# Reading the moving tile and writing the PSUM bank from the last column to the first, in the weight matmuls of a hybrid decoder layer

## The chip, the core and the metric

The kernel runs on one core of one Trainium2 chip. The metric is the device time of one execution in microseconds (us). The kernel before takes 705.18 us, the median of three runs (705.11 to 707.22 us).

## What is computed

One decoder layer over 512 tokens of width 1024, float32 in and out. Cut to what matters here:

```python
h = rms_norm(x, mix_norm_g)
proj = h @ w_in                      # 1024 x 3864
u, q, kv, nsa_g, merge_g = split(proj)
y_pool = pooling_mixer(u, pool_w, pool_scale) @ w_pool_out
y_nsa = nsa_mixer(q, kv, ...) @ w_nsa_out
x = x + (gate_pool * y_pool + gate_nsa * y_nsa) @ w_out
h = rms_norm(x, ffn_norm_g)
gate_pre, val = split(h @ w_up)      # 1024 x 5632
gate_c = causal_dwconv(gate_pre, conv_w, conv_b)
x = x + (silu(gate_c) * val) @ w_down   # 2816 x 1024
```

The products with `w_in`, `w_pool_out`, `w_nsa_out`, `w_out`, `w_up` and `w_down` are dense and take most of the arithmetic. The sparse attention inside `nsa_mixer` is computed as dense causal attention with masks, beside a compressed branch.

## The kernel before, in words

**Layout.** Activations lie transposed: 128 features on the partitions, 512 tokens along the free dimension. A dense product takes a 128x128 block of weights as the stationary operand and a 128x512 tile of activations as the moving operand, and adds up over the blocks of the contraction in one PSUM bank of 512 float32 columns.

**Three products for one.** Each float32 operand is split into a rounded part (names ending in `h` or `hi`) and the rest (`l`, `lo`), both of type fp32r. One block of the contraction is three matmuls: high weights by high activations, high by low, low by high. `mm3` (lines 439 to 446) issues these three for each block `k` into one bank `pt`. `weights` (lines 424 to 434) brings the weights from DRAM through the ring `wraw` and splits them into the rings `whi` and `wlo`, either with ScalarE (ACT) and VectorE (DVE), or with ACT and a DMA that adds on GpSimd's queue (POOL).

**Who calls `mm3`.** `feature` (22 outputs of `w_in`, 8 blocks each), `pool_out` (8 outputs, 4 blocks), the product with `w_nsa_out` (8 outputs, 4 blocks), the product with `w_out` (8 outputs, 8 blocks), `up_plain` (the first 4 of the 22 blocks of the feed-forward width, 2 outputs of 8 blocks each), `dn_group` (4 groups of 8 outputs, 4 blocks each) and the last product (8 outputs, 6 blocks). Each of these matmuls is 512 columns wide.

**Who calls `product`.** For the other 18 blocks of the feed-forward width, `up_fast` (from line 1178) computes the two outputs by a scheme that needs seven products of half width in the place of eight. `product` (lines 1133 to 1141) issues one of them: 4 blocks, three matmuls each, 256 columns wide, into the first 256 columns of a bank. Sums of weights are made on DVE beforehand; the moving tiles `nh`, `nl`, `th`, `tl` are sums and differences of the normalised activations, made once by `halves`.

**What else PE does.** TensorE (PE) also runs ten warm-up matmuls on a tile of ones, the projections `round_a` and the value projection (weights as the moving operand), the four matmul triples of `mix`, the compression matmuls (moving tile `kcb`, read with a step of 8 elements, 62 columns), attention scores, transposes and the products with the values (`av`). None of these is touched.

**What sets the order.** All instructions are first noted in a plan (`Plan.note`), then put in an order per engine by a small simulation (`Plan.run`) with a price for each instruction (`Plan.price`: for PE it is worked out from the number of columns of the moving operand alone) and with the dependences that `_span` finds from the footprint of every access pattern. `_span` takes steps below zero into account. `emit` then issues the instructions, all from line 382, so that every row of the profile reads L382 and groups are told apart by the names of their tiles: `mm<-xh,whi` writes a bank with the tag `mm` from the moving tile `xh` and the weights `whi`. The feed-forward weights come on SyncE's DMA queue (SP).

Of the kernel before, what the change touches and what calls it, by code (L numbers as in the profile page):

```python
# [385 lines left out]
def hybrid_layer(ctx: ExitStack, tc: tile.TileContext, xT, pos, par, cst, poolw, w1, wa, wb, wf,  # L386
# [3 lines left out]
    PE, ACT, DVE, POOL, SP = pl.engines  # L390
# [16 lines left out]
    def keep(name, shape, dt=F32, bufs=1):  # L407
        return pl.tile(sb, shape, dt, name, "t_" + name, bufs)

    def bank(tag, shape=(P, T)):  # L410
        return pl.tile(ps, shape, F32, tag, tag, {"mm": 2, "tr": 3, "av": 1, "sc": 1}[tag], psum=True)
# [12 lines left out]
    def weights(ap, width, lo="d"):  # L424
        raw, hi, low = ring("wraw"), ring("whi", F32R), ring("wlo", F32R)
        SP.dma_start(raw[:, :width], ap)
        if lo == "d":
            ACT.activation(low[:, :width], raw[:, :width], AF.Copy, scale=-1.0)
            POOL.dma_start(low[:, :width], raw[:, :width], accum_op=ALU.add)
            ACT.activation(hi[:, :width], raw[:, :width], AF.Copy)  # L430
        else:
            ACT.activation(hi[:, :width], raw[:, :width], AF.Copy)
            DVE.tensor_sub(low[:, :width], raw[:, :width], f32(hi[:, :width]))
        return hi, low

    def flat(ap):
        return ap.rearrange("p k n -> p (k n)")

    def mm3(pt, wh, wl, xh, xl, k0, k1, koff=0, nk=None, first=0):
        nk = k1 if nk is None else nk  # L440
        for k in range(k0, k1):
            c = slice((k - koff) * P, (k - koff + 1) * P)
            with pl.unit():
                PE.matmul(pt, wh[:, c], xh[k], start=(k == first), stop=False)
                PE.matmul(pt, wh[:, c], xl[k], start=False, stop=False)
                PE.matmul(pt, wl[:, c], xh[k], start=False, stop=(k == nk - 1))

    def rsqrt(dst, v, tmp):
        y, a = dst, tmp
# [32 lines left out]
    pt = bank("mm")  # L482
# [3 lines left out]
    xr, xh, xl = [None] * KD, [None] * KD, [None] * KD  # L486
# [113 lines left out]
    for c, (k0, k1) in enumerate(((0, 3), (3, 6), (6, 8))):  # L600
        raw = ring("wraw")
        SP.dma_start(raw[:, :(k1 - k0) * 280], flat(wb[:, k0:k1]))
        for j in range(k1 - k0):
            home = ("pp", 10) if len(bw) < 5 else ("pt", 6)
            hi, lo = (pl.tile(sb, (P, 280), F32R, n, home[0], home[1]) for n in ("bh", "bl"))
            split(hi, lo, raw[:, j * 280:(j + 1) * 280])
            bw.append((hi, lo))
    for t in range(NT):
        pt = bank("mm")
        tk = slice(t * P, (t + 1) * P)  # L610
        for k in range(KD):
            wh, wl = bw[k]
# [46 lines left out]
    for t in range(NT):  # L659
        x, y = qp[t], kp[t]  # L660
# [33 lines left out]
    def feature(i, hi, lo):  # L694
        wh, wl = weights(flat(wf[i]), 1024)
        pt = bank("mm")
        mm3(pt, wh, wl, hi, lo, 0, KD)
        return pt
# [8 lines left out]
    with pl.on("f"):  # L707
        for i in range(2):
            pt = feature(i, xh, xl)
# [48 lines left out]
        def pool_out(c):  # L758
            wh, wl = weights(wpo[c].rearrange("p a k n -> p (a k n)"), 1024)
            for f in (2 * c, 2 * c + 1):  # L760
                o = (f % 2) * 512
                pt = bank("mm")
                mm3(pt, wh[:, o:o + 512], wl[:, o:o + 512], yph, ypl, 0, 4)
                DVE.scalar_tensor_tensor(gpy[f], gpy[f], 1.0, pt, op0=ALU.add, op1=ALU.mult)
                SP.dma_start(gdr[f], gpy[f])
# [25 lines left out]
    for i in range(2):  # L791
# [4 lines left out]
        pt = bank("tr")  # L796
# [20 lines left out]
    x = keep("kcx", (64, 1, DH))  # L817
# [195 lines left out]
    def any_bank():  # L1013
        turn[0] += 1
        return bank(("mm", "tr", "tr", "mm", "tr", "av")[turn[0] % 6])

    mh, ml, nots = [], [], []
    for c in range(4):
        wh, wl = weights(wno[c].rearrange("p a k n -> p (a k n)"), 1024, "v")
        for f in (2 * c, 2 * c + 1):  # L1020
            o = (f % 2) * 512
            pt = any_bank()
            mm3(pt, wh[:, o:o + 512], wl[:, o:o + 512], Oh, Ol, 0, 4)
            nots.append(pl.last())
            m = page("tn")
            with pl.behind(tail):
                SP.dma_start(m, tdr[f])
            DVE.scalar_tensor_tensor(m, m, 1.0, pt, op0=ALU.add, op1=ALU.mult)
            gp = page("gp")
            with pl.behind(tail):  # L1030
                SP.dma_start(gp, gdr[f])
            DVE.tensor_add(m, m, gp)
            hi, lo = page("mh", dt=F32R), page("ml", dt=F32R)
            ACT.activation(hi, m, AF.Copy, scale=0.5)
            DVE.scalar_tensor_tensor(lo, m, 0.5, f32(hi), op0=ALU.mult, op1=ALU.subtract)
            mh.append(hi)
            ml.append(lo)
            if f > 1:
                tail = nots[f - 2]
# [4 lines left out]
    for f in (0, 4, 1, 5, 2, 6, 3, 7):  # L1044
        xres = page("xres")
        with pl.behind(tail):
            SP.dma_start(xres, xT[f])
        wh, wl = weights(flat(wout[f]), 1024, "v")
        pt = any_bank()
        mm3(pt, wh, wl, mh, ml, 0, KD)  # L1050
        tail = pl.last()
        x2[f] = pl.tile(sb, (P, T), F32, "x2", "pp", 10)
        DVE.tensor_add(x2[f], pt, xres)
        gh[f], gl[f] = page("gh", dt=F32R), page("gl", dt=F32R)
        split(gh[f], gl[f], x2[f], ffng[:, f:f + 1])
        if f:
            sq = page("sq")
            ACT.activation(sq, x2[f], AF.Square)
            DVE.tensor_add(acc, acc, sq)
        else:  # L1060
            ACT.activation(acc, x2[f], AF.Square)
# [3 lines left out]
    H2 = T // 2  # L1065
# [67 lines left out]
    def product(bank_, a, b, k0):  # L1133
        ah, al = a
        bh, bl = b
        for k in range(4):
            c = slice(k * P, (k + 1) * P)
            with pl.unit():
                for j, (w, x) in enumerate(((ah, bh), (ah, bl), (al, bh))):
                    PE.matmul(bank_[:, :H2], w[:, c], x(k), start=k0 and k == 0 and j == 0,  # L1140
                              stop=k == 3 and j == 2, skip_group_check=True)

    def mov(i, half):
# [34 lines left out]
    def up_fast(f, n1, n2, n3):  # L1178
# [30 lines left out]
        p1, u2, u3 = half[0][:, :H2], half[0][:, H2:], half[1][:, :H2]  # L1209
        g, y = page("fg"), page("y")  # L1210
        product(bx, halves_(a1, 0), mov(0, 0), True)
        begun.append(pl.last())
        ACT.activation(p1, bx[:, :H2], AF.Copy)
        more = list(held)
        del held[:]
        if more:
            more[0]()
        fill(n1, f == PLAIN)
        product(by, h2, mov(2, 1), True)
        DVE.tensor_add(u2, by[:, :H2], p1)  # L1220
        if more:
            more[1]()
        fill(n3)
        product(bq, h1, mov(2, 0), True)
        product(bx, halves_(a1, 1), mov(1, 0), False)
        ACT.activation(g[:, :H2], bx[:, :H2], AF.Copy)
# [31 lines left out]
    for f in range(8):  # L1258
        wh, wl = weights(flat(wdz[f]), 768, "v")
        pt = any_bank()  # L1260
# [99 lines left out]
```

## Time and profile before

| | us |
|---|---|
| Median of three runs | 705.18 |
| The profiled execution | 706.15 |
| Its span, from the first to the last instruction | 704.4 |
| PE busy in it | 697.2 |
| LDWEIGHTS (PEld) busy, beside PE | 615.6 |
| DVE busy | 492.7 |
| ACT busy | 422.3 |
| POOL busy | 103.7 |

The profiled execution is 0.97 us above the median of the runs, and 1.75 us of it lie outside the span. A busy share says how much of the span an engine had an instruction in flight. [...] What a matmul costs in a dense row is the distance from its start to the next start. This is called its pace below.

### The profile page before, as it was taken

The page shows a single profiled execution, that of the slowest core. Times are in us where ns is not written, and L with a number is a line of the kernel's source. Part 1 is how long each engine was busy: PE and PEld are TensorE (multiplying, and loading weights), DVE is VectorE, ACT ScalarE, POOL GpSimd, SP SyncE. Part 2 cuts the span into 40 slices and gives each one's busy share as a digit, 9 for nine tenths or more (in the row PEclk, how much of TensorE's full clock was granted, in tenths as well). Part 3 has the DMA queues.
Part 4 walks back from the last instruction along what each step waited for, and adds up shares of the span by engine and source line. Part 5 has one row for each costly group of instructions (what it writes and reads, how often), then busy time and mean ns, then how long its engine had stood idle before and what let it go on. Part 6 is the DMA issues. An engine that isn't in the chain of part 4 may idle for free.

```text
span 704.4 us, 11308 instructions
## 1 busy us (share of the span) xinstructions
PE 697.2 (99%) x4142; PEld 615.6 (87%) x4142; DVE 492.7 (70%) x1060; ACT 422.3 (60%) x756; POOL 103.7 (15%) x127
## 2 busy tenths in 40 slices
PE   9999999999999999999999999999999999999997
PEld 8898888888888888888888899999989999999886
DVE  6768488887866653675569967886778777776632
ACT  8557367677776664333467857685757566673310
POOL 0001301010110000000021323231312112220000
PEclk9999999999999999999999999999999999999999
DMA  8477255454565567844369698989868666774131
GB/s 297 167 180 224 61 120 135 105 132 109 150 153 143 146 139 229 280 158 156 122 150 235 151 211 170 219 185 222 186 173 205 157 162 166 170 161 112 45 127 60
DMA packets 45272, 113.99 MB, mean 162 GB/s; under 512 B 5281, under 2 KB 5409, under 8 KB 45217
## 3 DMA queue, kind: packets, MB, share of 16 engines
q1 hardware_dynamic: 29232, 76.57, 33.6%
q0 software_dynamic: 15840, 36.71, 29.1%
q8 instruction: 32, 0.52, 0.3%
q14 instruction: 24, 0.19, 0.1%
q10 hardware_dynamic: 144, 0.01, 0.0%
HBM read 70.27 MB, written 6.29 MB: 109 GB/s over the span
## 4 chain that ended last, share of the span: by engine, by line
PE 88%; DMA 3%; issue 3%; DVE 3%; ACT 1%; POOL 1%; POOLq 0%; ACTq 0%; DVEq 0%
PE mm L382 39%; PE tr L382 28%; PE sc L382 12%; PE av L382 10%; DMA sl<-r 2%; DMA r<-wup 1%; DVE wlo L382 1%; DMA sl<-wraw 0%; ACT whi L382 0%; DVE y L382 0%; POOL tl L382 0%; POOL sl L382 0%; ACT ft L382 0%; ACT sh L382 0%; DVE kc L382 0%
## 5 line engine op out<-in xcount | busy, mean ns | idle before, releaser
L382 ACT ACTIVATE whi<-wraw 128x1024 fp32r<-128x1024 f32 (+1 forms) x96 | 97.9, 1019 | 74.4 <-issue 29.0
L382 DVE TENSOR_TENSOR wlo<-wraw,whi 128x1024 fp32r<-128x1024 f32 (+1 forms) x66 | 76.4, 1157 | 16.6 <-ACT whi L382 14.3
L382 POOL DMA_DIRECT2D wlo<-wraw x30 | 26.3, 875 | 332.0 <-ACT wlo L382 278.7
L382 PE MATMUL mm<-xh,whi 128*128 128x512 f32 x176 | 73.0, 415 | 0.3
L382 PE MATMUL mm<-xh,wlo 128*128 128x512 f32 x176 | 69.0, 392 | 0.0
L382 PE MATMUL mm<-xl,whi 128*128 128x512 f32 x176 | 69.0, 392 | 0.0
L382 PE MATMUL mm<-tl,sh 128*128 128x256 f32 x190 | 53.8, 283 | 0.0
L382 PE MATMUL mm<-th,sh 128*128 128x256 f32 x174 | 49.5, 285 | 1.3 <-DVE u L382 1.2
L382 PE MATMUL mm<-th,sl 128*128 128x256 f32 x174 | 49.3, 284 | 0.2 <-DMA sl<-r 0.2
L382 POOL DMA_DIRECT2D sl<-r x36 | 31.4, 872 | 72.8 <-ACT sl L382 46.7
L382 ACT ACTIVATE pp<-pp,asm 128x128 f32<-128x128 f32 (+3 forms) x64 | 35.4, 556 | 11.1 <-DVE asm L382 11.0
L382 DVE SCALAR_TENSOR_TENSOR ft<-fg,pr,ft 128x511 f32<-128x511 f32 (+1 forms) x44 | 33.0, 749 | 11.8 <-ACT ft L382 11.1
L382 PE MATMUL sc<-yh,whi 128*128 128x512 f32 x104 | 40.8, 392 | 0.0
L382 PE MATMUL sc<-yl,whi 128*128 128x512 f32 x104 | 40.8, 392 | 0.0
L382 ACT ACTIVATE wlo<-wraw 128x1024 fp32r<-128x1024 f32 x30 | 31.8, 1060 | 14.9 <-PE mm L382 6.0
L382 PE MATMUL sc<-yh,wlo 128*128 128x512 f32 x104 | 40.5, 389 | 0.0
L382 PEld LDWEIGHTS mm<-xh,wlo 128*128 128x128 f32 x176 | 33.0, 188 | 7.3
L382 PEld LDWEIGHTS mm<-xh,whi 128*128 128x128 f32 x176 | 33.2, 189 | 5.8 <-DVE th L382 1.0
L382 PEld LDWEIGHTS mm<-xl,whi 128*128 128x128 f32 x176 | 33.3, 189 | 4.0
L382 PEld LDWEIGHTS mm<-tl,sh 128*128 128x128 f32 x190 | 36.4, 192 | 0.4
L382 PEld LDWEIGHTS mm<-th,sh 128*128 128x128 f32 x174 | 33.2, 191 | 3.1 <-DVE u L382 1.9
L382 ACT ACTIVATE ft<-fg,pr 128x512 f32<-128x512 f32 x22 | 17.8, 811 | 27.6 <-DVE fg L382 22.0
(394 smaller groups left out, 2116.9 us busy)
## 6 DMA issues: line engine op xcount, KB each, us to landing
wlo<-wraw POOLq DMA_DIRECT2D x30, 512.0 KB, 4.5
wraw<-wup SPq DMA_DIRECT2D x26, 512.0 KB, 4.3
wraw<-wf SPq DMA_DIRECT2D x22, 512.0 KB, 3.4
r<-wup SPq DMA_DIRECT2D x36, 256.0 KB, 4.7
sl<-r POOLq DMA_DIRECT2D x36, 256.0 KB, 5.3
wraw<-wdn SPq DMA_DIRECT2D x16, 512.0 KB, 4.5
sl<-s POOLq DMA_DIRECT2D x18, 256.0 KB, 6.2
sl<-wraw POOLq DMA_DIRECT2D x18, 256.0 KB, 4.3
```

The lines of the kernel that those rows point to most:

```text
L382: getattr(self.real[o.eng], method)(*a, **kw)
```

## The change

`back` turns a flat two-dimensional access pattern round: the offset becomes that of the last column and the step becomes -1. In `mm3` and in `product` the moving operand and the output in PSUM are both turned round, so that column n-1 is read first and written first, and column 0 last. Each output column still belongs to the same input column. The stationary operand (the weights), the number of matmuls, their sizes, the flags and all other instructions are as before.

```diff
+    def back(x):
+        n = x.ap[1][1]
+        return bass.AP(tensor=x.tensor, offset=x.offset + n - 1, ap=[list(x.ap[0]), [-1, n]])
+
     def mm3(pt, wh, wl, xh, xl, k0, k1, koff=0, nk=None, first=0):
...
             with pl.unit():
-                PE.matmul(pt, wh[:, c], xh[k], start=(k == first), stop=False)
-                PE.matmul(pt, wh[:, c], xl[k], start=False, stop=False)
-                PE.matmul(pt, wl[:, c], xh[k], start=False, stop=(k == nk - 1))
+                PE.matmul(back(pt), wh[:, c], back(xh[k]), start=(k == first), stop=False)
+                PE.matmul(back(pt), wh[:, c], back(xl[k]), start=False, stop=False)
+                PE.matmul(back(pt), wl[:, c], back(xh[k]), start=False, stop=(k == nk - 1))
...
     def product(bank_, a, b, k0):
...
                 for j, (w, x) in enumerate(((ah, bh), (ah, bl), (al, bh))):
-                    PE.matmul(bank_[:, :H2], w[:, c], x(k), start=k0 and k == 0 and j == 0,
+                    PE.matmul(back(bank_[:, :H2]), w[:, c], back(x(k)), start=k0 and k == 0 and j == 0,
                               stop=k == 3 and j == 2, skip_group_check=True)
```

## The prediction

> **What bounds the kernel now.** I began with the page's head and its first two parts, which say how much of the span each engine was busy and at which clock TensorE ran.
>
> ```profile
> span 704.4 us, 11308 instructions
> PE 697.2 (99%) x4142; PEld 615.6 (87%) x4142; DVE 492.7 (70%) x1060; ACT 422.3 (60%) x756; POOL 103.7 (15%) x127
> PE   9999999999999999999999999999999999999997
> PEclk9999999999999999999999999999999999999999
> ```
>
> PE had a matmul in flight for 697.2 of 704.4 us, in every slice and at the full granted clock. No other engine is near that. Busy matmuls overlap, so I looked next at whether PE ever waits: the chain that ended last, and the waits of PE.
>
> ```profile
> PE 88%; DMA 3%; issue 3%; DVE 3%; ACT 1%; POOL 1%; POOLq 0%; ACTq 0%; DVEq 0%
> ```
>
> ```profile
> PE mm L382 <- DVE u L382: 1.2, 2, 0.6
> PE mm L382 <- POOL ones L382: 1.0, 1, 1.0
> PE tr L382 <- DVE qs L382: 0.2, 1, 0.2
> PE tr L382 <- ACT qt L382: 0.2, 1, 0.2
> PE mm L382 <- DMA sl<-r: 0.2, 1, 0.2
> ```
>
> The waits come to 2.8 us (1.2 + 1.0 + 0.2 + 0.2 + 0.2), and 1.0 of it is the start. So the kernel is one long row of matmuls, and its time is the pace of that row. The pace is read from the timeline of PE in two dense stretches: 19 rows of 512 columns, and 27 rows of 256 columns, of which the first and the last stand here.
>
> ```profile
> 299.75 0.39 PE L382 MATMUL mm<-ol,whi 128*128 128x512 f32 x1
> ...
> 303.83 0.39 PE L382 MATMUL tr<-ol,whi 128*128 128x512 f32 x1
> ```
>
> ```profile
> 599.74 0.28 PE L382 MATMUL tr<-nh,sh 128*128 128x256 f32 x1
> ...
> 602.86 0.28 PE L382 MATMUL tr<-nh,wlo 128*128 128x256 f32 x1
> ```
>
> 512 columns: (303.83 - 299.75) / 18 = 226.7 ns from start to start. 256 columns: (602.86 - 599.74) / 26 = 120.0 ns. One more column therefore costs (226.7 - 120.0) / 256 = 0.4167 ns, and what is left over is a fixed gap of 226.7 - 512 x 0.4167 = 13.3 ns for each matmul. These two numbers carry the rest.
>
> **The change, part by part.** How many matmuls it touches follows from the loops. With 512 columns: 22 x 8 + 8 x 4 + 8 x 4 + 8 x 8 + 8 x 8 + 32 x 4 + 8 x 6 = 544 blocks (the callers of `mm3` in the order of the text above), three matmuls each, 1632. With 256 columns: 18 x 7 x 4 x 3 = 1512. Together 3144 of PE's 4142 instructions. Two groups fit the loops: the first is 22 x 8, and the second is a part of the 1512, by bank and tile.
>
> ```profile
> L382 PE MATMUL mm<-xh,whi 128*128 128x512 f32 x176 | 73.0, 415 | 0.3
> L382 PE MATMUL mm<-tl,sh 128*128 128x256 f32 x190 | 53.8, 283 | 0.0
> ```
>
> In columns: 1632 x 512 + 1512 x 256 = 1,222,656. At 0.4167 ns that is 509.4 us of streaming, and 3144 gaps of 13.3 ns are 41.9 us more: 551 of the 704.4 us are touched.
>
> Nothing is removed, added or moved beside this. The planner prices a matmul by its number of columns, which stays, and a pattern that runs backwards has the same footprint, so the order on all five engines and on the SP and POOL queues should stay, with the same waits. What can change is the time of one column and the time of one gap. No row of this trace has a backward pattern, so I bound the price by neighbours.
>
> *Rows that say a single element at a time is slower.* ScalarE and VectorE stream the same memories:
>
> ```profile
> L382 ACT ACTIVATE whi<-wraw 128x1024 fp32r<-128x1024 f32 x80 | 84.4, 1054 | 48.2 <-issue 29.0 <-PE mm L382 5.6 <-PE tr L382 5.1
> L382 ACT ACTIVATE sh<-wraw 128x512 fp32r<-128x512 f32 x36 | 22.4, 621 | 7.0 <-DVE wraw L382 6.4 <-ACT sh L382 0.6
> L382 DVE TENSOR_TENSOR x<-sc,x 128x512 f32<-128x512 f32 x26 | 17.9, 690 | 9.8 <-PE sc L382 9.7
> L382 DVE TENSOR_TENSOR u<-mm,u 128x256 f32<-128x256 f32 x34 | 14.4, 422 | 9.8 <-PE mm L382 8.6
> L382 DVE TENSOR_TENSOR kc<-mm,rb 64x256 f32<-64x256 f32 x8 | 3.4, 422 | 0.1
> ```
>
> ACT takes (1054 - 621) / 512 = 0.846 ns for an element, DVE (690 - 422) / 256 = 1.047 ns. PE takes 0.4167 ns, half of ACT's time. An estimate from that ratio: PE handles two neighbouring float32 columns in one step of about 0.83 ns, and a backward pattern, whose next element lies below, may lose the pairing on the read or on the accumulating write. Then a column costs 0.833 ns.
>
> *Rows that say a step costs nothing.* The `kc` rows read a PSUM bank with a step of 2 elements, and take the 422 ns of the `u` rows, which read it without a gap. And PE itself has one moving tile with a step of 8 elements:
>
> ```profile
> L382 PE MATMUL tr<-kcb,w 128*128 128x62 f32 x64 | 8.0, 293 | 0.0
> L382 PE MATMUL tr<-cs,pp 128*128 128x128 f32 x160 | 24.3, 272 | 0.0
> ```
>
> ```profile
> 74.83 1.99 PE L382 MATMUL tr<-kcb,w 128*128 128x62 f32 x16
> ```
>
> ```profile
> 170.47 0.71 PE L382 MATMUL tr<-cs,pp 128*128 128x128 f32 x5
> ```
>
> Sixteen stepped ones start every (1.99 - 0.293) / 15 = 113 ns, against (0.71 - 0.272) / 4 = 110 ns for dense transposes of 128 columns. Both look set by something other than columns (the load of the next weights, presumably), so the stepped read says only that a column costs at most 113 / 62 = 1.82 ns.
>
> So the price of a backward column lies between nothing extra and 1.82 - 0.417 = 1.41 ns; in time between 0 and 1.41 x 1,222,656 = 1720 us. DVE's step would give 0.63 ns or 771 us, ACT's 0.43 ns or 525 us, a lost pairing exactly 0.4167 ns or 509 us. These ends are far apart. I take the lost pairing: the row nearest in kind is a stream of float32 at one element a step, and ACT's slope is within 2% of it. The DVE row with a step is nearer in pattern, but it runs at 1.047 ns for each element, where there is no pairing to lose.
>
> [...]
>
> **Sum.** Against the profiled execution: 706.15 + 509.4 = 1215.6. PE is then later than what it waits for now, so the 1.4 us of waits on `u` and on the DMA of `sl` go: 1214.2. The DMA queues and the other engines move nothing more and have 509 us more time; DVE's 492.7 us lie beside it all, so no other engine can become the bound. In the terms of the median of the runs, 0.97 us lower: **1213 us**. Own range 1195 to 1235: at ACT's slope instead, 525 us more than 706.15 less 1.4 and 0.97 is 1229; and gaps that overlap with a slower stream may give some of the 41.9 us back.
>
> **The rivals.**
>
> *Order is free: 705 us.* If the memory only looks at whether the next element lies in the line just opened, a backward row hits each line as often as a forward one, and the pace stays 226.7 and 120.0 ns. The step-2 rows of DVE speak for it; the ratio to ACT's slope speaks against it. The same result comes if the instruction is built so that nothing is turned round, since both sides are turned together. [...]
>
> *A dearer gap: 747 us.* The column price stays, but starting at the far end costs a second gap, 3144 x 13.3 ns = 41.9 us. For it speaks that a gap exists; against it that the weights, not the moving tile, change with each matmul.
>
> *The gap closes: 667 us.* The fixed 13.3 ns may be a turn-round, from the last column of one matmul to the first of the next, that belongs to the forward direction. Without it 512 columns take 213.3 ns; 256 columns can only fall to the 110 ns that rows with quick columns show. That is 1632 x 13.3 + 1512 x 10.5 ns = 37.6 us, hence 705.2 - 37.6 = 667.6. It happens on PE in all stages after the first projections, and it decides from 0.67 ns for each matmul on (0.3% of 705 us over 3144). Against it: the gap is the same for both widths and in all banks, which fits a change of weights better.
>
> *Other column prices.* Three steps for two columns: +255 us, 959. One element at the pace of DVE or up to the bound of the stepped read: 1475 to about 2425.
>
> **How the numbers follow.** About 0.3% is what a measurement of this kernel can tell from no change. Chances: lost pairing 0.46; free order 0.12; dearer gap 0.10; three steps for two 0.06; dearer columns 0.08; gap closing wholly or partly 0.18, of which 0.06 lies between 690 and 703 us. Faster 0.18, same 0.12, slower 0.46 + 0.10 + 0.06 + 0.08 = 0.70. A range from 690 to 1235 holds 0.46 + 0.12 + 0.10 + 0.06 + 0.06 = 0.80. It is wide because a column's price is either untouched or doubled, and the trace has no row of the kind.
>
> **What would show it right or wrong.** If the pairing is lost, the profile after has starts of 512 columns about 440 ns apart and of 256 columns about 227 ns, while the first 40 us (the untouched projections) and the transposes keep their pace; PE stays the bound, with fewer waits, at a granted clock still in the nines. Two paces again give the column price and the gap separately, and so tell a dearer gap (both paces up by the same ns) from dearer columns (512 up by twice as much as 256). Wrong would be a pace within 0.7 ns of before: then the order of columns is nothing that this memory sees. Any change of time with unchanged paces would have to come from waits, which I hold to be untouched.

## The result and the profile after

The changed kernel takes 713.18 us, the median of four runs (711.56 to 713.64), beside 706.02 us for four runs of the kernel before (705.11 to 707.22). The ratio is 1.0096, with a 95% interval of 1.0071 to 1.0121: slower by about 1%, or 7 us. 1213 us was forecast. The profiled execution after took 711.56 us, with a span of 709.8 us; before it was 704.4 us, so 5.4 us are to be found in the two traces.

The page after, its line of busy time and its chain:

```profile
PE 702.3 (99%) x4142; PEld 613.0 (86%) x4142; DVE 493.3 (70%) x1060; ACT 422.5 (60%) x756; POOL 103.7 (15%) x127
PE 97%; DVE 1%; DMA 1%; issue 0%; ACT 0%; POOL 0%; DVEq 0%; ACTq 0%; POOLq 0%
```

They show the same row of matmuls, as many of them, 5.1 us longer in busy time, and still the bound. PE's waits hardly differ; the longest of before has grown by 0.6 us, and the wait on the DMA of `sl` is gone:

```profile
PE mm L382 <- DVE u L382: 1.8, 2, 1.2
```

The order of the instructions on PE, DVE, ACT and POOL's queue is unchanged, as was forecast. What moved is the pace. These are the timelines of PE after in dense stretches like those of before: the first and last of 23 rows of 512 columns, and of 36 rows of 256 columns.

```profile
298.75 0.40 PE L382 MATMUL av<-ol,whi 128*128 128x512 f32 x1
...
303.88 0.40 PE L382 MATMUL mm<-oh,wlo 128*128 128x512 f32 x1
```

```profile
601.81 0.28 PE L382 MATMUL mm<-th,sh 128*128 128x256 f32 x1
...
605.96 0.28 PE L382 MATMUL tr<-th,sl 128*128 128x256 f32 x1
```

512 columns: (303.88 - 298.75) / 22 = 233.2 ns, 6.5 ns more than before. 256 columns: (605.96 - 601.81) / 35 = 118.6 ns, 1.4 ns **less** than before. Two widths moved in opposite directions. Summed over all distances from one start to the next in the two traces: the 1007 wide ones from the product with `w_nsa_out` on lose 5.9 us (229.3 to 235.1), the 528 of `feature` 2.0 us, the 96 of `pool_out` 0.2, the 1512 of `product` win 2.6 us. The untouched 96 matmuls of the value projection (280 columns) are 0.5 us shorter after; an experiment below shows that this is not the change's doing. All the other untouched ones together lose 0.4 us. 5.9 + 2.0 + 0.2 - 2.6 - 0.5 + 0.4 = 5.4 us, the difference of the spans. `feature` loses less for each matmul because its forward pace, among attention matmuls, was a median of 230 ns and not 226.7; backward it is 233 there too.

### The profile page after: what moved, and what is told of

The parts are those of the page before. It is cut to its first block, busy times and chain, and to the rows that moved or that the text cites. A ratio compares the mean times of both kernels' runs of the same rounds, so it can differ in the third digit from the quotient of the medians.

```text
span 709.8 us, 11320 instructions
## 1 busy us (share of the span) xinstructions
PE 702.3 (99%) x4142; PEld 613.0 (86%) x4142; DVE 493.3 (70%) x1060; ACT 422.5 (60%) x756; POOL 103.7 (15%) x127
## 4 chain that ended last, share of the span: by engine, by line
PE 97%; DVE 1%; DMA 1%; issue 0%; ACT 0%; POOL 0%; DVEq 0%; ACTq 0%; POOLq 0%
PE mm L382 41%; PE tr L382 31%; PE sc L382 13%; PE av L382 11%; DMA r<-wup 1%; DVE kc L382 0%; DVE th L382 0%; DVE u L382 0%; DVE o L382 0%; DVE x L382 0%; DVE y L382 0%; ACT ft L382 0%; DVE ks L382 0%; DVE qs L382 0%; ACT qs L382 0%
```

## The experiments

### Which part of the change, and which side of it

Theory W: the sign hangs on the width. Theories R and P: the read of the moving tile sets the new pace, or the write to PSUM. Four kernels undo a part of the change each.

`mm3_only`: `product` is as before.

```diff
-PE.matmul(back(bank_[:, :H2]), w[:, c], back(x(k)), ...
+PE.matmul(bank_[:, :H2], w[:, c], x(k), ...
```

> Only the 512-column matmuls of mm3 run backwards; the 256-column ones of product run forward. Theory W (the sign of the effect hangs on the width): the profile after shows 512 columns at about 233.2 ns (226.7 before) and 256 columns at about 118.5 ns (120.0 before), so this kernel should lose 1632 x 6.5 ns = 10.6 us against before, more than the full change lost, and 256 columns should be back at 120.0 ns. Rival C (the paces differ because the executions differ, not the direction): this kernel is within 2 us of the full change's 713 us and 256 columns stay near 118.5 ns though they run forward.

Measured: 715.12 us against 706.59 (15 runs), ratio 1.0115, interval 1.0101 to 1.0129. In its trace the wide ones are a median of 233 ns apart and the 256-column ones 120 again. The loss of 8.5 us is 2 us below the expectation, which counted `feature` and `pool_out` at the dense pace. Rival C falls: 256 columns forward went back to 120.0 ns.

`product_only`: `mm3` is as before, `product` backward.

```diff
-PE.matmul(back(pt), wh[:, c], back(xh[k]), ...     # and the two others
+PE.matmul(pt, wh[:, c], xh[k], ...
```

> Only the 256-column matmuls of product run backwards; mm3 is as before. Theory W: 1512 x 1.5 ns = 2.3 us faster than before, about 703.5 us, with 512 columns at 226.7 ns and 256 columns at 118.5 ns. Rival C: no gain; 256 columns at 120.0 ns or the 512-column pace moves too.

Measured: 703.99 us, ratio 0.9964, interval 0.9951 to 0.9976: a gain of 2.6 us. In its trace 256 columns have a median of 117 ns and 512 columns of 227. In the profiled execution alone the waits of PE on `u` are 3.6 us, against 1.2 before, and take back what the pace gave there: the 1512 distances sum to 184.2 us, waits included, against 183.9 before. That the median won by as much as expected is therefore not fully shown to be the pace.

`read_only` reads backward and writes forward; `write_only` reads forward and writes backward.

```diff
-PE.matmul(back(pt), wh[:, c], back(xh[k]), ...
+PE.matmul(pt, wh[:, c], back(xh[k]), ...           # read_only, all three, and in product
+PE.matmul(back(pt), wh[:, c], xh[k], ...           # write_only, all three, and in product
```

> All touched matmuls read the moving tile backwards but write PSUM forward, so the tokens come out in reverse order and what follows computes on other numbers; the work is the same. Theory R (the read from SBUF sets the new pace): 512 columns at 233.2 ns, 256 at 118.5 ns, time about that of the full change. Theory P (the write to PSUM sets it): paces as before, 226.7 and 120.0 ns, time within 1 us of before.

> All touched matmuls write PSUM backwards but read forward; the tokens come out in reverse order, the work is the same. Theory R: paces as before, 226.7 and 120.0 ns. Theory P: 512 columns at 233.2 ns, 256 at 118.5 ns, time about that of the full change.

Measured: 711.78 us, ratio 1.0078 (1.0062 to 1.0093), for the backward read; 706.67 us, ratio 1.0000 (0.9990 to 1.0010), for the backward write. The timelines of PE in the dense stretch, 19 rows each; first `read_only`, then `write_only`:

```profile
309.63 0.40 PE L382 MATMUL tr<-oh,wlo 128*128 128x512 f32 x1
...
313.83 0.40 PE L382 MATMUL mm<-mh,wlo 128*128 128x512 f32 x1
```

```profile
309.77 0.39 PE L382 MATMUL mm<-mh,wlo 128*128 128x512 f32 x1
...
313.85 0.39 PE L382 MATMUL tr<-mh,wlo 128*128 128x512 f32 x1
```

4.20 / 18 = 233.3 ns and 4.08 / 18 = 226.7 ns. The backward write costs nothing that this interval can show, and the backward read alone has the pace of the full change. Theory R holds, P falls.

### How much two executions of one kernel differ

`before_again` is the kernel before without an edit.

> The kernel before, unchanged, profiled once more, to see how far the paces of one kernel move between two executions. All theories: 226.7 ns at 512 and 120.0 ns at 256 columns in the dense stretches. If the untouched matmuls of 280 columns, 133 ns apart in the first profile and 126 to 131 ns in the changed kernel, differ here too, they vary by execution and not by the change.

Measured: 705.29 us, beside 704.97 for the run of before with it. The paces are those of the first profile, 227 and 120 ns, but for the 96 matmuls of 280 columns: they took 12.88 us in the first profile of before and 12.35 us in this one. The two values come again to the hundredth in the other kernels (12.88 in `mm3_only`, 12.35 after the change). The same instructions in the same order run at one of two paces.

### Sections of matmuls by themselves

`micro` keeps nothing of the layer. It loads the tiles once and runs sections like this one, named by direction of read and write and by width:

```python
for k in range(24):
    PE.matmul(wr(pt[:, :n]), whi[:, c], rd(xh[k % 8][:, at:at + n]), start=(k == 0), stop=(k == 23))
```

> The layer is left out; the kernel only runs sections of 48 matmuls (in two banks) with the same weights and tiles, with no transfer and no other engine beside them, and names each section by direction of read and write (f forward, b backward) and by width. Theory R with a rate (a backward read costs a little more for each column, and its start a little less): ffa, fba (512) 226.7 ns, bba, bfa 233.2 ns; ffb, fbb (256) 120.0 ns, bbb, bfb 118.5 ns; 384 columns 173.3 forward and 175.9 backward, 320 columns 146.7 and 147.2, 448 columns 200.0 and 204.5, so that the two cross near 300 columns. Theory S (a step between widths, such as a fixed extra stall once more than 256 columns are read backwards): 320 columns already lose about 6.6 ns. Theory X (the backward read only meets other engines or transfers differently): with nothing beside them forward and backward have equal paces at each width.

The timeline of PE merges the 48 matmuls of a section into one row (start, length, ..., count). The pace is the distance from the start of a section to that of the next, divided by 48.

```profile
27.64 11.04 PE L382 MATMUL ffa<-xh,whi 128*128 128x512 f32 x48
38.52 11.37 PE L382 MATMUL bba<-xh,whi 128*128 128x512 f32 x48
49.73 11.37 PE L382 MATMUL bfa<-xh,whi 128*128 128x512 f32 x48
60.93 11.06 PE L382 MATMUL fba<-xh,whi 128*128 128x512 f32 x48
71.82 5.92 PE L382 MATMUL ffb<-xh,whi 128*128 128x256 f32 x48
77.58 5.85 PE L382 MATMUL bbb<-xh,whi 128*128 128x256 f32 x48
83.26 5.84 PE L382 MATMUL bfb<-xh,whi 128*128 128x256 f32 x48
...
94.69 8.49 PE L382 MATMUL ffc<-xh,whi 128*128 128x384 f32 x48
103.02 8.70 PE L382 MATMUL bbc<-xh,whi 128*128 128x384 f32 x48
111.55 7.21 PE L382 MATMUL ffd<-xh,whi 128*128 128x320 f32 x48
118.59 7.21 PE L382 MATMUL bbd<-xh,whi 128*128 128x320 f32 x48
125.63 9.89 PE L382 MATMUL ffe<-xh,whi 128*128 128x448 f32 x48
135.36 10.08 PE L382 MATMUL bbe<-xh,whi 128*128 128x448 f32 x48
145.28 5.91 PE L382 MATMUL ffu<-xh,whi 128*128 128x256 f32 x48
```

| Columns | forward, ns | backward, ns |
|---|---|---|
| 256 | 120.0 | 118.3 |
| 320 | 146.7 | 146.7 |
| 384 | 173.5 | 177.7 |
| 448 | 202.7 | 206.7 |
| 512 | 226.7 | 233.5 |

Beside them there is no load or store, and of the other engines only DVE copies four columns after every 24 matmuls; the mean granted clock of this execution was 0.981. The paces are those of the full layer all the same: Theory X falls. Neither a price for each column nor a step between widths fits the table: 320 columns lose nothing, 384 lose 4 ns, and 448 are already 2.7 ns above the forward rule, which gives 200.0. Theory S falls as well.

`micro_b` changes the order of the read in finer ways. Each section is an access pattern of [step, count] pairs, for example `lba`, lines of four float32 (16 bytes) downwards with their elements upwards, and `iba`, the other way round. Such a group of four is called a line here:

```python
lba = bass.AP(..., offset=x.offset + 508, ap=[partitions, [-4, 128], [1, 4]])
iba = bass.AP(..., offset=x.offset + 3,   ap=[partitions, [4, 128], [-1, 4]])
```

> The layer is left out, as in the first kernel of sections; all sections write PSUM forward and 512 columns wide unless said. Measured so far: 512 columns 226.7 ns forward, 233.3 ns with the read backward. Theory L (lines: the read opens 16-byte lines, and pays when the next line lies below): lines in descending order with ascending elements inside (lba) 233.3 ns, elements descending inside ascending lines (iba, and jba in pairs) 226.7 ns. Theory E (elements: each step below costs, whatever the lines do): iba 233.3 ns or more, lba below it. Theory T (tile ends: the pace hangs on where one read ends and the next begins): two ascending halves in descending order (hfa) and descending inside ascending halves (hba) differ from both, and reading one and the same tile with each matmul (fxa forward, bxa backward) changes the difference of 6.6 ns. Theory V (overlap with the weight load): with the weights always from the same place (fwa, bwa) the difference changes. If none of that matters, fxa, fwa stay at 226.7 and bxa, bwa at 233.3 ns. A step of 2 elements (saa, 256 columns, two elements to a line) and of 4 elements (sab, 128 columns, one to a line) and a step of 0 (zaa) show what lines cost in a forward read: if lines matter, sab is well above the 110 ns of dense rows and saa above 120 ns.

```profile
116.99 11.04 PE L382 MATMUL iba<-xh,whi 128*128 128x512 f32 x48
127.87 11.37 PE L382 MATMUL lba<-xh,whi 128*128 128x512 f32 x48
139.08 11.06 PE L382 MATMUL jba<-xh,whi 128*128 128x512 f32 x48
...
172.07 10.52 PE L382 MATMUL zaa<-xh,whi 128*128 128x512 f32 x48
182.43 5.92 PE L382 MATMUL ibb<-xh,whi 128*128 128x256 f32 x48
...
193.87 11.21 PE L382 MATMUL saa<-xh,whi 128*128 128x256 f32 x48
204.90 5.88 PE L382 MATMUL sab<-xh,whi 128*128 128x128 f32 x48
210.58 5.95 PE L382 MATMUL fbb<-xh,whi 128*128 128x256 f32 x48
```

Elements downwards inside ascending lines (`iba`): 226.7 ns, as forward. Lines downwards with ascending elements (`lba`): 233.5 ns, as backward. Theory L holds: **the order of the lines counts, the order inside a line does not.** The same tile or the same weights with each matmul changed nothing (`fxa` to `bwa`, 227 and 233 ns). `zaa` reads one element again and again and takes 215.8 ns. So the "fixed gap" of 13.3 ns was no fixed gap: 10.9 ns of it go when the read moves through no lines.

`saa` (a step of 2) takes 229.8 ns for 256 columns, 0.90 ns for a column, and `sab` (a step of 4) 118.3 ns for 128, 0.92 ns; forward it is 120.0 / 256 = 0.47 ns. So a step can double the price of a column, as a lost pairing would; but a step of -1 does not.

`micro_c` asks whether the read meets the load of the next weights. It gives the stationary operand a step of 0 (`z`) or of 4 (`p`), and starts the moving tile one line later (`fma`, `bma`).

```python
PE.matmul(pt[:, :n], bass.AP(..., ap=[partitions, [0, 128]]), rd(xh[k % 8][:, 0:n]), ...)   # z
```

> The layer is left out; sections of 48 matmuls as before. So far a moving tile with step 0 (one line) takes 216 ns at 512 columns, a forward one 226.7, one with lines descending 233.3. Theory V (what is above 216 ns is the meeting of the moving lines with the lines that the next weight load reads): with a stationary operand of step 0 (fwz, bwz, and fvz, bvz at 256 columns) forward and backward fall to the same pace near 216 ns, and near 110 ns at 256; with a stationary operand of one column to a line (fwp, bwp, step 4, four times the lines) both rise. Theory M (the moving read alone costs it, at its start or at its end): fwz stays at 226.7 and bwz at 233.3 ns, fwp and bwp too. Where the moving tile starts (one line later, fma and bma, or 16 lines later, fmb and bmb) should then not matter in either; 288 and 480 columns (fna, bna, fnb, bnb) fill the table of widths: if the loss sat in the columns alone, 480 would lose about 6 ns and 288 nothing.

```profile
50.65 11.29 PE L382 MATMUL fwz<-xh,whi 128*128 128x512 f32 x48
61.78 11.36 PE L382 MATMUL bwz<-xh,whi 128*128 128x512 f32 x48
...
105.12 5.60 PE L382 MATMUL fvz<-xh,whi 128*128 128x256 f32 x48
110.56 5.82 PE L382 MATMUL bvz<-xh,whi 128*128 128x256 f32 x48
...
121.57 11.64 PE L382 MATMUL fwp<-xh,whi 128*128 128x512 f32 x48
133.05 11.36 PE L382 MATMUL bwp<-xh,whi 128*128 128x512 f32 x48
144.25 5.77 PE L382 MATMUL fma<-xh,whi 128*128 128x256 f32 x48
149.86 5.92 PE L382 MATMUL bma<-xh,whi 128*128 128x256 f32 x48
155.62 5.91 PE L382 MATMUL fmb<-xh,whi 128*128 128x256 f32 x48
```

The loads of the weights with step 4 and step 0, from the page (the second figure behind the first bar is the mean of one in ns):

```profile
L382 PEld LDWEIGHTS fwp<-xh,whi 128*128 128x128 f32 x48 | 11.4, 316 | 0.0
L382 PEld LDWEIGHTS fwz<-xh,whi 128*128 128x128 f32 x48 | 9.1, 189 | 2.1
```

Neither theory came through whole. The forward pace depends on how the weights are read: 231.9 ns at 512 and 113.3 ns at 256 columns with step 0 (226.7 and 120.0 with plain weights), 239.2 ns with step 4. The backward pace at 512 stays at 233.3 with weights of step 0 and of step 4 (`bwz`, `bwp`). With step 4 a load itself takes longer (316 ns), so step 0 is the cleaner evidence: the loads of `fwz` take 189 ns, as plain ones do (188 to 189 ns for `mm<-xh,wlo` and `mm<-xl,whi` in the kernel before), and still 512 columns take 5 ns more (`fwz`) and 256 columns 7 ns less (`fvz`). That the two reads meet in the memory is argued from this, not shown. Yet 216 ns was not reached, so the weights are not all of it. Two more widths in this kernel do not fit a loss in the columns alone: 288 columns take 131.7 ns forward and 133.3 backward, 480 take 216.7 and 220.0. And one line later the signs are swapped: 116.9 ns forward, 120.0 backward. That pointed away from direction, to place.

`micro_d` moves the start of one wide tile through 0 to 64 columns; its last sections move the start of the weights instead.

> The layer is left out; sections of 48 matmuls that read one wide tile from a start moved by 0 to 64 columns (second letter f: 512 columns, s: 256 columns; third letter a 0, b 1, c 2, d 4, e 8, f 12, g 16, h 20, i 24, j 28, k 32, l 64), forward (first letter f) or backward (b), or with the weights moved by 4 or 16 columns (w). One line later has swapped the signs at 256 columns: 116.9 ns forward, 120.0 backward, where 119.7 and 118.3 stood before. Theory A (where a read starts and ends sets the pace, and backward only swaps the two ends): forward paces vary with the start by several ns and come back with a period; some start gives 512 columns forward about 233 ns, some gives backward about 227 ns, and some gives less than 226.7. Theory D (direction itself costs): 512 columns stay at 226.7 ns forward and 233.3 backward wherever they start.

```profile
28.57 11.04 PE L382 MATMUL ffa<-xw,whi 128*128 128x512 f32 x48
39.45 11.52 PE L382 MATMUL ffb<-xw,whi 128*128 128x512 f32 x48
50.80 11.35 PE L382 MATMUL ffc<-xw,whi 128*128 128x512 f32 x48
...
179.22 5.60 PE L382 MATMUL fsd<-xw,whi 128*128 128x256 f32 x48
184.66 5.77 PE L382 MATMUL fse<-xw,whi 128*128 128x256 f32 x48
...
274.71 11.37 PE L382 MATMUL wfg<-xw,whi 128*128 128x512 f32 x48
```

Forward, 512 columns take 226.7 ns from column 0, 236.5 from column 1, 229 to 234 from columns 2 to 32, and 227.1 again from column 64. 256 columns take 119.8 from column 0, 123.1 from column 1 and 113.3 from column 4. Theory A holds against D: a forward read can be slower than the backward one, and at 256 columns clearly faster than from column 0. It has two misses: backward stays at 233.3 to 233.5 ns from all three starts tried, and no forward start gives 512 columns less than 226.7. Of the twelve starts tried, column 0 was the best at 512 columns, with the pace of the kernel before. The place of the weights counts too: with the moving tile at column 0, read forward, and the weights starting 16 columns later (`wfg`; the next section starts at 285.92), 512 columns take 233.5 ns, the backward pace; with the weights 4 columns later they stay at 227.1.

`micro_e` reads the aligned tile in other orders of its lines.

> The layer is left out; sections of 48 matmuls that read an aligned tile in other orders of its 16-byte lines, ascending inside each line (names p, a letter for the order, s for 256 or f for 512 columns; a is the plain forward order, b swaps neighbouring lines, c interleaves the two halves, d reads even lines and then odd ones, e odd lines and then even ones, f and g every fourth line, h every eighth, i every sixteenth, j every second line downwards, k blocks of 16 lines downwards, l downwards inside blocks of 16 lines, m and n the same with blocks of 8). Theory A (the places of the lines set the pace, direction is one case of it): the orders differ among each other by several ns, some lie above 233.3 ns or below 226.7 at 512 columns, and some below 118.3 at 256. Theory D (only going down costs): a, c, d, f, h, i stay at 226.7 and 120.0 ns, and j, and b, e, g, k, l, m, n in part, lie towards 233.3.

```profile
33.67 5.63 PE L382 MATMUL pbs<-xh,whi 128*128 128x256 f32 x48
39.13 6.25 PE L382 MATMUL pcs<-xh,whi 128*128 128x256 f32 x48
...
175.85 10.82 PE L382 MATMUL pgf<-xh,whi 128*128 128x512 f32 x48
186.51 11.97 PE L382 MATMUL phf<-xh,whi 128*128 128x512 f32 x48
```

Neighbouring lines swapped (`pbs`): 113.8 ns at 256 columns. Sweeps of every fourth line, the last of four first (`pgf`): 222.1 ns at 512, below the forward 226.7; the same orders at the other width are 232.9 and 115.8. Every sixteenth line is the worst, 276 and 135 ns. Both directions occur among the good and the bad orders: Theory A again.

### Versions of the layer with better orders

`product_pairs` gives `product` the swapped pairs; `both_orders` also gives `mm3` the sweeps; both read and write in the new order, so each result lands where it did.

```diff
+def pairs(x):     # offset + 4,  [8, n // 8], [-4, 2], [1, 4]
+def fourths(x):   # offset + 12, [-4, 4], [16, n // 16], [1, 4]
-PE.matmul(bank_[:, :H2], w[:, c], x(k), ...
+PE.matmul(pairs(bank_[:, :H2]), w[:, c], pairs(x(k)), ...
-PE.matmul(pt, wh[:, c], xh[k], ...
+PE.matmul(fourths(pt), wh[:, c], fourths(xh[k]), ...      # both_orders only, all three
```

> The whole layer, with product reading its 256 columns and writing PSUM with the two 16-byte lines of each pair swapped (columns 4 to 7, 0 to 3, 12 to 15, 8 to 11 and so on), mm3 as before. Theory A (the places of the lines set the pace, and PSUM's order costs nothing): 256 columns 113.3 ns in place of 120.0, hence 1512 x 6.6 = 10 us faster than before, about 696 us, and faster than with product backward. Rival G (a PSUM order in groups of four costs, which no section tried): slower than that by as much as the write takes, up to no gain or a loss. Rival D (only going down costs, every second line goes down here): 118 to 120 ns and at most 2 us.

> As the kernel with product in swapped pairs, and mm3 reads its 512 columns and writes PSUM in four sweeps of every fourth line, the last line of each four first. Theory A: 512 columns 222.2 ns in place of 226.7 in the dense stretches, 1104 x 4.5 = 5 us, and about as much less again where they stand among other matmuls, so 3 to 7 us faster than the kernel with pairs alone, about 690 us. Rival G: a write order in such sweeps costs more than it gains, and this kernel is slower than the one with pairs alone.

Measured: 701.34 us (ratio 0.9934, interval 0.9920 to 0.9949) and 697.83 us (0.9882, 0.9870 to 0.9895), beside 706.09. Both win, but 5 and 8 us short of the expected times; the sweeps add 3.5 us to the gain of the pairs, within the 3 to 7 expected. In `product_pairs` the 256-column median is 113 ns, as expected, but not throughout: there are stretches at 120, two of them 55 and 57 matmuls long, that begin in the middle of a row of pairs. And PE now waits 3.7 us for DVE's work on `u`. In `both_orders` the sweeps hold (222 ns at 512), but the very same pairs run at a median of 120 ns.

`micro_f` puts 48 matmuls of 256 columns behind 24 of 512 in different orders. `qcs` are pairs, read and written, behind forward ones, `qgs` the same behind sweeps.

```python
section("qgf", 512, fourths, fourths, reps=1)
section("qgs", 256, pairs, pairs)
```

> The layer is left out; 24 matmuls of 512 columns (names ending in f) run ahead of 48 of 256 columns (ending in s). Ahead: forward in a to d and j, in sweeps of every fourth line in e to i, backward in k and l. The 256 columns are read forward (a, e), in swapped pairs with a forward write (b, f) or a write in pairs (c, g, k), backward (d, h, l), in sweeps of fourths (i, j). Theory K (the pace is a rhythm between the reads of the moving tile and of the next weights that is carried over from what ran before): the same 256-column order has different paces behind different neighbours, pairs about 113 ns behind forward and 120 ns behind sweeps. Theory W2 (the write order of the pairs costs what was missing): pairs take 113 ns in b and f and 120 ns in c, g and k. Theory O (only the order of the reads counts): 113 ns in b, c, f, g and k alike, 118 in d, h and l, 116 in i and j; then what was missing in the full layer comes from something that these sections leave out.

```profile
56.51 5.60 PE L382 MATMUL qcs<-xh,whi 128*128 128x256 f32 x48
61.95 5.60 PE L382 MATMUL qdf<-xh,whi 128*128 128x512 f32 x24
...
100.32 5.92 PE L382 MATMUL qgs<-xh,whi 128*128 128x256 f32 x48
106.08 5.49 PE L382 MATMUL qhf<-xh,whi 128*128 128x512 f32 x24
```

The same instructions on the same tiles: 113.3 ns and 120.0 ns, each steady from the second matmul on. With a forward write behind sweeps (`qfs`) the trace starts at 120 and 116 ns and settles at 113; behind backward ones (`qks`) it goes through 119 and 121 to 113. Write order alone does not decide (`qcs` and `qks` write in pairs at 113). Theory K fits in part: one order of reads can run at two steady paces, as the 280-column matmuls did. What picks the pace is not shown. The neighbour alone does not: behind the same sweeps, pairs settle at 113 ns with a forward write (`qfs`) and at 120 with a write in pairs (`qgs`), and in `product_pairs` both paces occur though every `mm3` matmul there reads forward. Each section ran once, so the write order behind sweeps, or chance, may have a part in it.

`sweeps_all` then gives `product` the sweeps too.

```diff
-PE.matmul(pairs(bank_[:, :H2]), w[:, c], pairs(x(k)), ...
+PE.matmul(fourths(bank_[:, :H2]), w[:, c], fourths(x(k)), ...
```

> The whole layer, with both mm3 and product reading and writing in sweeps of every fourth 16-byte line (the last of each four first). Theory K (pace is a rhythm that can settle in more than one state): 256 columns in sweeps took 115.6 ns behind both kinds of neighbour, so product should leave the 120 ns that its pairs settled in behind sweeps; 1512 x 4.4 = 6.6 us less than the kernel with sweeps and pairs (697.8), some of it taken back by waits for DVE and the weights, so 691 to 695 us. Rival N (the 120 ns behind sweeps come from the full layer itself, from weights and tiles of other places): product stays at 120 ns and the time at 698 us.

```profile
PE 683.0 (99%) x4142; PEld 607.6 (88%) x4142; DVE 492.6 (71%) x1060; ACT 421.8 (61%) x756; POOL 103.4 (15%) x127
```

Measured: 694.59 us beside 706.76, ratio 0.9855, interval 0.9824 to 0.9886. 256 columns have a median of 116 ns, so it is not the layer that holds them at 120 ns: Rival N falls, and the time lies in the expected 691 to 695 us. PE's busy time is 14.2 us below that of before. This is the best version found, ahead of both kernels.

## Why the prediction was wrong

- **What bounds the kernel, what is touched, the order:** right. PE is the bound before and after, the order of the instructions stayed, and the loss lies in the pace of the touched matmuls. The waits were to fall by 1.4 us, since PE was to be much later; it was not, and the wait on `u` rose from 1.2 to 1.8 us while the one on `sl` went.
- **The price of a backward column: the step that failed.** The prediction saw that PE takes 0.4167 ns for a column and ACT 0.846 ns for an element, took that, as an estimate, for PE handling two columns at a time, and let a step of -1 lose the pair. No run shows that pairing. A step of 2 does about double the price (`saa`, 0.90 ns a column), as a lost pair would, but -1 does not: within a line of four the order of elements is free (`iba`, 226.7 ns). An access pattern that runs down touches the same lines with as many elements each. In place of 0.4167 ns more for each column, 512 columns cost 6.5 ns more in all and 256 columns 1.4 ns less. The ratio to another engine's speed was evidence on the engine, none on a step of -1.
- **The row of DVE with a step of 2** was set aside with the argument that DVE has no pairing to lose. That DVE and PE differ here was right: the `kc` rows took 422 ns with the step, as the `u` rows did without it, and 256 columns on PE 229.8 ns (`saa`) in place of 120.0. But neither says anything of a step of -1.
- **The fixed gap of 13.3 ns:** wrong as a thing of its own. At step 0, 10.9 ns of it are gone; in other orders of lines 512 columns take 222 to 276 ns, so that what is over 512 x 0.4167 = 213.3 ns runs from 9 to 63 ns. A straight line goes through any two widths; the widths between them (448 columns at 202.7 ns in place of 200.0) and the other orders do not lie on it.
- **The rivals.** *Order is free*, on its assumption about lines, gave 705 us. It fits the read inside a line (`iba`, 226.7 ns) and the write: at -1 it took no more time (`write_only`, ratio 1.0000), and sweeps that also write in sweeps keep their 222 ns. For the order of lines it is wrong by 7 us; orders that touch the same lines took 222 to 276 ns. *A dearer gap* forecast both paces up alike, which did not happen; and its reason against, that the moving tile does not change with each matmul, misread `mm3`, where `xh[k]` and `xl[k]` alternate (one tile throughout made no difference, `fxa` 227 ns). *The gap closes* was right in sign for 256 columns alone.
- **The range and the chances.** 713 us lies between 690 and 1235, but only since that range took in the other cases; the lost pairing's own range began at 1195. The sign was given 0.70, but most of that for a loss 70 times too large, so that the right sign is luck.

What stays open: why the pace of a moving read hangs on the order of its lines. The pattern and the place of the weight load have a part in it (`fwz`, `fvz`, `wfg`), the start and order of the lines too, and one order can have two paces; a model that gives 233.3 ns backward and 226.7 forward was not found.

## What to carry to other kernels

A dense row of matmuls should be read by its distance from start to start, at three widths or more and in more than one execution, before a gap in it is called fixed. A price that no row shows is best bounded by what the operation touches (here as many lines as before), not by the speed of another engine. Where TensorE is the bound, the start and the order of 16-byte lines in the moving read are worth a trial: reading and writing in sweeps took about 1.5% off this kernel with no other edit. The best order has to be tried in the kernel itself, since 256-column pairs at 113 ns alone ran at 120 ns beside sweeps.

## What the runs showed of the hardware that was not expected

- Backward elements inside a line are free (`iba` 226.7 ns), and so is a backward write to PSUM (`write_only` 1.0000).
- One start column later costs a 512-column read 9.8 ns (`ffb` 236.5 against 226.7); a start one line later saves 6.5 ns at 256 columns in the wide tile (`fsd` 113.3 against 119.8 for `fsa`).
- Weights that start 16 columns later raise a forward 512-column read from 226.7 to 233.5 ns (`wfg`).
- One order of lines can run at two steady paces, 113.3 and 120.0 ns; the 280-column matmuls of an unchanged kernel do so from one execution to the next (12.88 and 12.35 us).
